# Probabilities times V for two query blocks in one product of 256 columns

## The chip, the core and the metric

One NeuronCore of a Trainium2 chip runs the whole program. The metric is the time of one execution on the device in microseconds (us). The profile covers one execution and gives the span from its first to its last instruction. Engines: PE is the matrix engine (TensorE), PEld its loads of weights, DVE the vector engine, ACT the scalar engine, POOL is GpSimd, and SP issues most of the DMAs.

## What is computed

Two layers over 512 latent tokens (a grid of 8 rows by 64 columns) and 256 context tokens, width 1024. In each layer the normed tokens go through one projection into three groups of heads side by side: neighbourhood attention (4 heads of 64, called NA below), a state-space mixer in both directions (SSD) and attention with shared keys and values (4 query heads, 2 key heads, called GQA). One output projection joins them, then a SwiGLU block follows. The part that the change touches is the last line of each attention:

```python
def gqa_softmax_attention(q, k, v):
    s = jnp.einsum('bqgrd,bkgd->bgrqk', q, k) * (HEAD_DIM ** -0.5)
    p = jax.nn.softmax(s.astype(jnp.float32), axis=-1).astype(v.dtype)
    return jnp.einsum('bgrqk,bkgd->bqgrd', p, v)
```

Neighbourhood attention is the same over a window of keys with a bias and the context keys. Context tokens see context keys only. In the second layer the context tokens have no output.

## The kernel before

A scheduler puts each engine's instructions into one fixed order when the program is built; priorities follow the order in which the code is written, and a tile's buffers (a tag and a count) limit how far work runs ahead. On the chip each engine takes its own list in order and waits at semaphores.

Each layer has three stretches: projections, the attention stage, and the output projection with the feed-forward block. The attention stage of layer 0 takes 301 to 470 us of the span, that of layer 1 takes 1290 to 1423 us. In it the units of attention, the SSD core, the gate and the loads of the next stage are interleaved by a table (`UCFG`) that says at which unit each event is written.

`attn` handles two heads (`j`) and two blocks of 128 queries (`qi`), four units. Each layer calls it for two pairs of NA heads and two pairs of GQA heads, and for each pair for two halves of the tokens and, in layer 0, for the context: 20 calls in all, 12 in layer 0 and 8 in layer 1. A unit's `scores` (lines 390, 393) write to PSUM tile `S`; DVE takes the maximum; ACT writes exponentials to `pr` (line 410); POOL scales them (line 415). `transposes` turns `pr` by identity matmuls on PE into PSUM tile `PT` (line 424), and ACT or DVE copies that to SBUF (lines 428, 430): tiles `PHA` for head 0 and `PHB` for head 1, one for each block of queries. `values` (line 436) multiplies by V. It has V as the stationary operand, 64 columns of the array for each head (`tile_position`), so that head 0 uses the left half of the array and head 1 the right half, and 128 columns of transposed probabilities stream through for each of 5 (NA), 6 (GQA) or 2 (context) key tiles. Every product is float32 and appears in the trace as two passes. `yout` copies the result out of PSUM tile `sm`: for NA by ACT (lines 622, 625) with one DMA for both blocks, for GQA by `split` into a rounded part on ACT (line 282) and the rest on DVE (line 283).

The loop at lines 1095 to 1104 writes for unit i: scores of unit i+2, events, normalising of unit i+1, transposes of unit i, events, and then the pending product of the unit before:

```python
            units[i][2][2]()
            events(i + 0.5)
            if pend:
                pend()
            pend = units[i][2][3]
```

Other work that is spoken of: `diag` (SSD within a chunk) loads two tiles `wh`, `wl` from `crow` (line 884), forms decays on DVE (line 892) and multiplies on PE (lines 913, 914), whose end frees the two tiles for the next load; line 958 forms states and line 971 what tokens see of them, both full-array products of 256 columns. `mod_chunk` (line 178) multiplies modulation weights with 32 columns of the array for each of four products. `PHA` and `PHB` also hold four of the eight low parts of the normed tokens (`h_tiles`), and early on weights of the modulation.

Of the kernel before, what the change touches and what calls it, by code (L numbers as in the profile page):

```python
# [8 lines left out]
F32 = mybir.dt.float32  # L9
F32R = mybir.dt.float32r  # L10
# [4 lines left out]
P = 128  # L15
D = 1024
KB = 8
# [11 lines left out]
def hybrid_kernel(ctx: ExitStack, tc: tile.TileContext, a, out, dbg=None):  # L29
# [18 lines left out]
    HT = ["HY"] * 4 + ["HS"] * 4 + ["HZ"] * 4 + ["PHA"] * 2 + ["PHB"] * 2  # L48
    GT = ["GV"] * 2 + ["GX"] * 4 + ["GB"] * 2 + ["GT"] * 2 + ["GC"] * 2 + ["GK", "GR", "GR", "GR"]
    BUFS = {t: (XT + HT + GT).count(t) for t in XT + HT + GT}  # L50
    BUFS.update(XFB=2, YO=1, HD=1)
# [33 lines left out]
    class Split:  # L85
        """columns 0 .. 511 in one bank of PSUM, the others in another"""
# [20 lines left out]
    # ---------------------------------------------------------- constants  # L107
# [42 lines left out]
    # ---------------------------------------------------------- modulation  # L150
# [8 lines left out]
    def mod_loads(l, c, tags):  # L159
        """512 columns of the modulation weights in tiles of the given tags, one or two k per tile"""  # L160
        w, k = [], 0
        for tag in tags:
            if tag in WB:
                wt, n = T(sb, tag, WB[tag], [P, 2, 512]), 2
            else:
                wt, n = T(sb, tag, BUFS[tag], [P, 1, 512]), 1
# [6 lines left out]
    def mod_chunk(l, c, w):  # L173
        """columns 512 c .. 512 c + 511 of the modulation; four row groups of the array take four k"""
# [21 lines left out]
    def mod_rows():  # L196
        """silu of both conditioning vectors as rows on every partition, in four tiles (vector, half)"""
# [11 lines left out]
    def mod_dots(l, c, rows, ptile, aside):  # L209
        """the same columns as mod_chunk by products along rows of the transposed weights"""  # L210
# [50 lines left out]
    # ---------------------------------------------------------- helpers  # L261
# [26 lines left out]
    def h_tiles():  # L288
        return [slot(HT[d], F32R) for d in range(KB)], [slot(HT[8 + d], F32R) for d in range(KB)]

    def spread(rstd, n):
        """per-token values as a row on every partition"""
# [10 lines left out]
    def make_h(l, xT, h, pbs, part, shi, sc):  # L303
        """norm, scale and shift of one part of the tokens"""
# [25 lines left out]
    def proj_ws(pt, wh, wl, xh, xl, nk, segs, ks=None):  # L330
        """pt[:, seg] = W^T x, W stationary (nk blocks of 128 rows)"""
# [13 lines left out]
    def proj_as(pt, ws, n, kper, xh, xl, t):  # L345
        """pt[:, :n] = x[t]^T W, activations stationary"""
# [28 lines left out]
    def attn(V2, xk, kts, qcols, bias, yout):  # L375
        """two heads and two blocks of queries; xk: range of x keys (or None); kts: key tiles for P V.
        Returns the steps of the four units: scores and softmax, transposes, and P V where one is complete"""
# [39 lines left out]
        def transposes(j, qi):  # L417
            t_ = ph[j, qi] = slot("PH" + "AB"[j], F32, (P, 6, P))
# [13 lines left out]
        def values(qi):  # L432
# [60 lines left out]
    for l in range(L):  # L493
# [109 lines left out]
        def na_sets():  # L603
            for b in range(2):
# [7 lines left out]
                for half in range(nhalf):  # L612
                    yt = []

                    def yout(pv, qi, b=b, half=half, yt=yt):
                        if qi == 0:
                            yt.append(sb_())
# [753 lines left out]
```

## Time and profile before

| | us |
|---|---|
| median of 3 runs | 1846.74 (1846.3 to 1852.83) |
| span of the profiled execution | 1843.3 |
| PE busy in the span | 1737.0 (94%) |
| attention stage of layer 0: length, PE busy | 168.6, 149.98 |
| attention stage of layer 1: length, PE busy | 132.5, 119.05 |

The page gives no time of the profiled execution besides its span; the span lies 3.4 us below the median of the runs. PE has a record for each pass, its busy time counts overlapping passes once, and a pass in flight counts as busy, so a busy PE can still be slowed by gaps between starts. The chain is the work that ended last, followed back step by step; a piece in it runs from its own start or release to that of the next piece.

### The profile page before, as it was taken

The page shows a single profiled execution, that of the slowest core. Times are in us where ns is not written, and L with a number is a line of the kernel's source. Part 1 is how long each engine was busy: PE and PEld are TensorE (multiplying, and loading weights), DVE is VectorE, ACT ScalarE, POOL GpSimd, SP SyncE. Part 2 cuts the span into 40 slices and gives each one's busy share as a digit, 9 for nine tenths or more (in the row PEclk, how much of TensorE's full clock was granted, in tenths as well). Part 3 has the DMA queues.
Part 4 walks back from the last instruction along what each step waited for, and adds up shares of the span by engine and source line. Part 5 has one row for each costly group of instructions (what it writes and reads, how often), then busy time and mean ns, then how long its engine had stood idle before and what let it go on. Part 6 is the DMA issues. An engine that isn't in the chain of part 4 may idle for free.

```text
span 1843.3 us, 26677 instructions
## 1 busy us (share of the span) xinstructions
PE 1737.0 (94%) x10146; PEld 1478.4 (80%) x10146; DVE 1104.0 (60%) x2209; ACT 681.5 (37%) x1386; POOL 423.1 (23%) x429
## 2 busy tenths in 40 slices
PE   7987778989999999999999999999899999999998
PEld 3887667777878888888888887989677788888887
DVE  4559996877475555455654576587786743333334
ACT  5554555556344221121112224334555442232222
POOL 0488886654010000000000002241653100000000
PEclk9998889989989999999999999999999999999999
DMA  9542526433123334333443454342631323333332
GB/s 368 201 139 103 163 89 186 140 90 106 56 75 115 114 115 126 103 116 107 124 129 102 130 163 139 96 131 79 183 105 53 108 90 93 99 96 92 103 100 83
DMA packets 94319, 221.66 MB, mean 120 GB/s; under 512 B 18416, under 2 KB 26224, under 8 KB 94192
## 3 DMA queue, kind: packets, MB, share of 16 engines
q1 hardware_dynamic: 78096, 204.65, 35.6%
q10 hardware_dynamic: 16096, 15.31, 2.5%
q8 instruction: 80, 1.31, 0.3%
q14 instruction: 47, 0.39, 0.1%
HBM read 198.49 MB, written 21.43 MB: 119 GB/s over the span
## 4 chain that ended last, share of the span: by engine, by line
PE 76%; DVE 11%; DMA 5%; ACT 3%; issue 2%; POOL 2%; SPq 0%; ACTq 0%; DVEq 0%; POOLq 0%
PE S L338 61%; PE sm L436 3%; DVE MB L768 2%; DMA wl<-crow 2%; PE PT L424 2%; DVE wl L327 1%; PE PT L338 1%; PE PT L352 1%; PE sm L352 1%; DMA wr<-in_mod_wT_dram 1%; DVE wh L892 1%; PE S L390 1%; ACT wh L326 1%; PE sm L913 1%; PE sm L914 1%
## 5 line engine op out<-in xcount | busy, mean ns | idle before, releaser
L326 ACT ACTIVATE wh<-wr 128x1024 fp32r<-128x1024 f32 (+3 forms) x214 | 207.6, 972 | 732.2 <-PE S L338 542.4
L327 DVE TENSOR_TENSOR wl<-wr,wh 128x1024 fp32r<-128x1024 f32 (+3 forms) x214 | 250.0, 1169 | 174.0 <-ACT wh L326 171.6
L269 POOL TENSOR_TENSOR tiny<-tiny,mhalf 128x2 f32<-128x2 f32 (+2 forms) x17 | 28.7, 1688 | 1067.5 <-DVE tiny L1160 1020.3
L338 PE MATMUL S<-HY,wh 128*128 128x512 f32 (+1 forms) x716 | 214.0, 357 | 5.9 <-ACT HY L318 4.1
L338 PE MATMUL S<-HY,wl 128*128 128x512 f32 (+1 forms) x716 | 214.5, 357 | 0.0
L338 PE MATMUL S<-HZ,wh 128*128 128x512 f32 (+1 forms) x716 | 212.8, 355 | 0.8 <-DVE HZ L319 0.8
L338 PE MATMUL S<-HS,wl 128*128 128x512 f32 (+1 forms) x716 | 213.1, 355 | 0.0
L338 PE MATMUL S<-HS,wh 128*128 128x512 f32 (+1 forms) x716 | 211.1, 353 | 0.0
L231 DVE CUSTOM_DVE_ANT_0 PT<-wr,XFB 128x512 f32<-128x512 f32 x112 | 75.5, 715 | 179.8 <-DMA wr<-in_mod_wT_dram 179.8
L338 PEld LDWEIGHTS S<-HY,wh 128*128 128x128 f32 x716 | 119.8, 192 | 27.2 <-ACT HY L318 4.4
L338 PEld LDWEIGHTS S<-HZ,wh 128*128 128x128 f32 x716 | 118.2, 191 | 21.7 <-DVE HZ L319 2.2
L338 PEld LDWEIGHTS S<-HS,wh 128*128 128x128 f32 x716 | 118.8, 191 | 20.2
L338 PEld LDWEIGHTS S<-HY,wl 128*128 128x128 f32 x716 | 118.8, 191 | 18.8
L338 PEld LDWEIGHTS S<-HS,wl 128*128 128x128 f32 x716 | 118.0, 190 | 18.6
L338 PE MATMUL S<-PHA,wh 128*128 128x512 f32 (+1 forms) x358 | 106.4, 355 | 0.0
L338 PE MATMUL S<-PHB,wh 128*128 128x512 f32 (+1 forms) x358 | 105.0, 351 | 0.0
L338 PE MATMUL S<-GX,wh 128*128 128x512 f32 (+1 forms) x400 | 97.2, 349 | 0.4 <-DVE KA L1114 0.4
L415 POOL TENSOR_SCALAR pr<-pr,tiny 128x640 f32<-128x640 f32 (+2 forms) x80 | 69.3, 869 | 84.0 <-DVE tiny L414 64.3
L768 DVE SCALAR_TENSOR_TENSOR MB<-MA,c,MB 128x770 f32<-128x770 f32 (+1 forms) x64 | 85.3, 1333 | 1.4
L228 POOL TENSOR_TENSOR KA<-QN,XFB 128x512 f32<-128x512 f32 x48 | 73.9, 1546 | 44.3 <-ACT XFB L205 23.5
L424 PE MATMUL PT<-c,pr 128*128 128x128 f32 x384 | 66.5, 289 | 13.4 <-POOL pr L415 4.6
L1261 DVE TENSOR_TENSOR MB<-S,MA 128x768 f32<-128x768 f32 (+1 forms) x42 | 34.6, 823 | 72.6 <-PE S L338 72.5
(402 smaller groups left out, 3911.7 us busy)
## 6 DMA issues: line engine op xcount, KB each, us to landing
wr<-in_mod_wT_dram SPq DMA_DIRECT2D x56, 512.0 KB, 3.7
wr<-in_w_gate_dram SPq DMA_DIRECT2D x44, 512.0 KB, 3.5
wr<-in_w_up_dram SPq DMA_DIRECT2D x44, 512.0 KB, 3.5
wr<-in_w_blk_dram SPq DMA_DIRECT2D x28, 512.0 KB, 3.6
wr<-in_w_down_dram SPq DMA_DIRECT2D x32, 448.0 KB, 3.3
QN<-in_mod_wT_dram SPq DMA_DIRECT2D x48, 256.0 KB, 3.3
wr<-in_w_out_dram SPq DMA_DIRECT2D x32, 256.0 KB, 2.6
wr<-in_w_down_dram SPq DMA_DIRECT2D x16, 512.0 KB, 3.4
```

The lines of the kernel that those rows point to most:

```text
L228: G.tensor_tensor(out=p_, in0=wv, in1=x, op=ALU.mult)
L231: V.tensor_tensor_reduce(out=p_, in0=wv, in1=x, scale=1.0, scalar=0.0, op0=ALU.mult, op1=ALU.add, accum_out=acc[:, o : o + 1],)
L269: POW.tensor_tensor(out=y, in0=v, in1=mhalf[:, 0:n], op=ALU.pow)
L326: S.activation(hi, raw, AF.Copy)
L327: V.tensor_tensor(lo, raw, hi.bitcast(F32), ALU.subtract)
L338: ins = PE.matmul(pt[:, c0:c1], lhsT=w, rhs=xx[:, c0:c1], start=(k == (0 if len(order) == 1 else order[0]) and i == 0), stop=(k == (nk - 1 ...
L352: PE.matmul(pt[:, 0:n], lhsT=s, rhs=w[:, o : o + n], start=(k == 0 and i == 0), stop=(k == KB - 1 and i == 2),)
L415: G.tensor_scalar(out=p_, in0=p_, scalar1=m[:, 4:5], scalar2=1.0, op0=ALU.mult, op1=ALU.mult)
L424: PE.transpose(pt[:, k * P : (k + 1) * P], pr[j, qi][:, kk * P : (kk + 1) * P], ident)
L436: PE.matmul(pv[64 * j : 64 * j + 64, 0:P], lhsT=V2(kts[k], j), rhs=ph[j, qi][:, k, :], start=(k == 0), stop=(k == nkt - 1), tile_position= ...
L768: V.scalar_tensor_tensor(ac[:, 0:wid], cp[:, j : j + wid], convw[l][:, b, j : j + 1], ac[:, 0:wid], ALU.mult, ALU.add)
L1261: V.tensor_tensor(gg[:, c0:c1], pu[:, c0:c1], sg[:, c0:c1], ALU.mult)
```

## The change

`values` runs once for each pair of heads, after the transposes of both query blocks, with 256 columns streaming instead of 128. The transposed probabilities of a head lie in one tile of two blocks (`PH`, three buffers of two blocks each, where `PHA` and `PHB` had two buffers of one block each). `yout` copies 256 columns at once. The low parts of normed tokens and the early modulation weights use halves of `PH`. A scratch area for DMA descriptors is made smaller; comments are gone, so line numbers behind line 170 differ by up to six.

```diff
-    HT = ["HY"] * 4 + ["HS"] * 4 + ["HZ"] * 4 + ["PHA"] * 2 + ["PHB"] * 2
+    HT = ["HY"] * 4 + ["HS"] * 4 + ["HZ"] * 4 + ["PH"] * 4
...
-    BUFS.update(XFB=2, YO=1, HD=1)
+    BUFS.update(XFB=2, YO=1, HD=1, PH=3)
...
-            if tag in WB:
-                wt, n = T(sb, tag, WB[tag], [P, 2, 512]), 2
+            if tag in WB or tag == "PH":
+                wt, n = T(sb, tag, WB.get(tag, 3), [P, 2, 512]), 2
...
-        return [slot(HT[d], F32R) for d in range(KB)], [slot(HT[8 + d], F32R) for d in range(KB)]
+        hi, lo = ([slot(HT[8 * i + d], F32R) for d in range(4 if i else KB)] for i in range(2))
+        for _ in range(2):
+            t = slot("PH", F32R, (P, 2, NT))
+            lo += [t[:, 0, :], t[:, 1, :]]
+        return hi, lo
...
-            t_ = ph[j, qi] = slot("PH" + "AB"[j], F32, (P, 6, P))
+            if qi == 0:
+                ph[j] = slot("PH", F32, (P, 2, 6, P))
+            t_ = ph[j][:, qi]
...
-        def values(qi):
+        def values():
             pv = ps_sm()
             for k in range(nkt):
                 for j in range(2):
                     PE.matmul(
-                        pv[64 * j : 64 * j + 64, 0:P], lhsT=V2(kts[k], j), rhs=ph[j, qi][:, k, :],
+                        pv[64 * j : 64 * j + 64, 0:256], lhsT=V2(kts[k], j), rhs=ph[j][:, :, k, :],
                         start=(k == 0), stop=(k == nkt - 1), tile_position=(0, 64 * j),
                     )
-            yout(pv, qi)
+            yout(pv)
...
-             lambda j=j, qi=qi: transposes(j, qi), (lambda qi=qi: values(qi)) if j else None, j)
+             lambda j=j, qi=qi: transposes(j, qi), values if j and qi else None, j)
...
-                            ov = yv.rearrange("p r c -> p c r")[:, 16 * qi : 16 * qi + 16, :]
-                            S.activation(ov, pv[:, 0:P].rearrange("p (c r) -> p c r", r=8), AF.Copy)
+                            S.activation(
+                                yv.rearrange("p r c -> p c r"), pv[:, 0:256].rearrange("p (c r) -> p c r", r=8), AF.Copy
+                            )
...
-                        split(yh[k][:, o : o + P], yl[k][:, o : o + P], pv[:, 0:P])
+                        split(yh[k][:, o : o + 256], yl[k][:, o : o + 256], pv[:, 0:256])
```

The scheduler gives a new order in both attention stages. PE's lists hold 384 products of line 436 before and 192 of line 442 now. These stand in 84 unbroken runs before and in 51 now.

First place: PE in layer 0, the first product of a pair of NA heads. Before, one of the two query blocks (result `sm_3111`) stands as one early product, not shown, and these two runs with transposes between them:

```order
L436 MATMUL sm_3111<-PHB_3060,GV_1042 64x128
L436 MATMUL sm_3111<-PHA_2998,GV_1042 64x128
L436 MATMUL sm_3111<-PHB_3060,GV_1042 64x128
L436 MATMUL sm_3111<-PHA_2998,GV_1042 64x128
L436 MATMUL sm_3111<-PHB_3060,GV_1042 64x128
L436 MATMUL sm_3111<-PHA_2998,GV_1042 64x128
L424 MATMUL PT_3093<-c_66,pr_3020 128x128 x2
L436 MATMUL sm_3111<-PHB_3060,GV_1042 64x128
L436 MATMUL sm_3111<-PHA_2998,GV_1042 64x128
L436 MATMUL sm_3111<-PHB_3060,GV_1042 64x128
L390 MATMUL S_3173<-KA_2861,QN_2858 128x384
```

Now both blocks together (result `sm_3139`), again behind one early product that is not shown:

```order
L442 MATMUL sm_3139<-PH_3053,GV_1036 64x256
L442 MATMUL sm_3139<-PH_2992,GV_1036 64x256
L442 MATMUL sm_3139<-PH_3053,GV_1036 64x256
L442 MATMUL sm_3139<-PH_2992,GV_1036 64x256
L442 MATMUL sm_3139<-PH_3053,GV_1036 64x256
L442 MATMUL sm_3139<-PH_2992,GV_1036 64x256
L430 MATMUL PT_3126<-c_66,pr_3044 128x128 x2
L442 MATMUL sm_3139<-PH_3053,GV_1036 64x256
L442 MATMUL sm_3139<-PH_2992,GV_1036 64x256
L442 MATMUL sm_3139<-PH_3053,GV_1036 64x256
L430 MATMUL PT_3166<-c_66,pr_3076 128x128 x3
```

The two runs cover one query block before and both blocks now; the second block's own two runs, which came next before, are gone.

Second place: PE in layer 0, the first product of `diag` (lines 913, 914 before, 915, 916 now; result tile `sm`, operands `MA`, `wh`, `wl`). Before:

```order
L424 MATMUL PT_3147<-c_66,pr_3051 128x128 x2
L436 MATMUL sm_3160<-PHB_3087,GV_1042 64x128
L436 MATMUL sm_3160<-PHA_3024,GV_1042 64x128
L436 MATMUL sm_3160<-PHB_3087,GV_1042 64x128
L393 MATMUL S_3215<-KA_2852,QN_2849 128x256
L393 MATMUL S_3215<-KB_2855,QN_2849 128x256
L913 MATMUL sm_3205<-MA_3108,wh_2992 128x64
L914 MATMUL sm_3205<-MA_3108,wl_2993 128x64
L913 MATMUL sm_3205<-MA_3108,wh_2992 128x64
```

Now:

```order
L960 MATMUL PT_3046<-XFB_3002,GB_2240 128x256
L960 MATMUL PT_3046<-XFB_3002,GB_2322 128x256
L442 MATMUL sm_3139<-PH_2992,GV_1036 64x256
L915 MATMUL sm_3184<-MA_3100,wh_2986 128x64
L916 MATMUL sm_3184<-MA_3100,wl_2987 128x64
L915 MATMUL sm_3184<-MA_3100,wh_2986 128x64
L916 MATMUL sm_3184<-MA_3100,wl_2987 128x64
L915 MATMUL sm_3184<-MA_3100,wh_2986 128x64
L916 MATMUL sm_3184<-MA_3100,wl_2987 128x64
```

Before, it stands behind all runs of the first pair's two query blocks (the last one is in the rows); now it stands behind one early product only, ahead of the pair's other nine.

Third place: SP in layer 0, loads of decays (`crow`, line 884 before, 886 now) among loads of keys and queries and of the bias table (`in_rpb_dram`). Before:

```order
L597 DMA GR_3548<-in_rpb_dram 128x384 x2
L884 DMA wh_3388<-crow_2527 128x512
L884 DMA wl_3389<-crow_2530 128x512
L358 DMA KA_3358<-nk_920 64x768 x2
L358 DMA KB_3361<-nk_922 64x768 x2
L358 DMA QN_3885<-gq_2076 64x768
L358 DMA QN_3885<-gq_2078 64x768
L358 DMA KA_3367<-nk_920 64x768 x2
L358 DMA KB_3370<-nk_922 64x768 x2
L358 DMA QN_3888<-gq_2076 64x768
L358 DMA QN_3888<-gq_2078 64x768
L884 DMA wh_3516<-crow_2527 128x512
```

Now:

```order
L886 DMA wh_3353<-crow_2521 128x512
L886 DMA wl_3354<-crow_2524 128x512
L603 DMA GR_3505<-in_rpb_dram 128x384 x2
L362 DMA KA_3323<-nk_914 64x768 x2
L362 DMA KB_3326<-nk_916 64x768 x2
L362 DMA QN_3814<-gq_2070 64x768
L362 DMA QN_3814<-gq_2072 64x768
L886 DMA wh_3474<-crow_2521 128x512
L886 DMA wl_3475<-crow_2524 128x512
L362 DMA KA_3332<-nk_914 64x768 x2
L362 DMA KB_3335<-nk_916 64x768 x2
L362 DMA QN_3817<-gq_2070 64x768
```

The two loads of a chunk stand one load of the bias table earlier in the first case, and between the keys of the two heads in the second.

## Rows read from the trace of the kernel before

**Rows 1.** The page: span, and the chain that ended last, by engine.

```profile
span 1843.3 us, 26677 instructions
...
PE 76%; DVE 11%; DMA 5%; ACT 3%; issue 2%; POOL 2%; SPq 0%; ACTq 0%; DVEq 0%; POOLq 0%
```

**Rows 2.** Windows of both attention stages: busy us of each engine, PEclk, DMA.

```profile
301.40:470.00 168.60, 149.98 (x1116) 120.42 (x1116) 128.58 (x359) 100.26 (x281) 94.65 (x123) 0.95 0.39 117
1290.50:1423.00 132.50, 119.05 (x896) 94.57 (x896) 99.27 (x262) 75.32 (x194) 70.00 (x88) 0.97 0.39 114
```

**Rows 3.** Line 436: one group of its matmuls, and one idle time ahead.

```profile
L436 PE MATMUL sm<-PHA,GV x176: 272/273/472, 303.9 to 1360.2; 128*64 128x128 f32 x176
...
  ACT PHB L428: 2.3, 2
```

**Rows 4.** The chain at 404 to 414 us: start, length, engine, line, instructions.

```profile
404.51 1.45 PE sm L436 x22
...
408.79 0.81 PE sm L436 x12
409.59 0.48 PE PT L424 x3
...
411.31 0.33 PE PT L424 x3
411.64 0.87 PE PT L971 x4
...
413.15 0.22 PE sm L913 x2
```

**Rows 5.** The chain in 301 to 470 us, its shares by line.

```profile
by line: PE sm L436 16.4%; PE PT L424 11.3%; DMA wl<-crow 7.3%; PE S L390 6.7%; PE S L393 5.3%; PE sm L913 5.1%; PE sm L914 5.0%; DVE wh L892 4.6%; PE S L338 4.1%; DMA zsp<-SA 3.7%; PE PT L971 3.5%; PE PT L958 3.3%; issue 2.8%; ACT pr L410 
```

**Rows 6.** The chain in 1290 to 1423 us, its shares by line.

```profile
by line: PE sm L436 15.9%; DMA wl<-crow 13.0%; PE PT L424 11.3%; DVE wh L892 7.1%; PE S L390 5.6%; PE S L338 5.1%; PE PT L958 3.9%; PE sm L913 3.9%; PE sm L914 3.8%; DVE tiny L407 3.4%; PE PT L971 3.4%; POOL HY L920 3.0%; issue 2.6%; PE S L
```

**Rows 7.** The chain in the first half of the first attention stage.

```profile
324.14 0.58 PE sm L436 x6
...
327.40 4.11 DMA wl<-crow
```

**Rows 8.** The chain in the first half of the second attention stage.

```profile
1306.21 2.32 PE sm L436 x18
...
1314.58 6.09 DMA wl<-crow
```

**Rows 9.** Windows of 20 us: busy us of each engine, PEclk, DMA.

```profile
380.00:400.00 20.00, 16.05 (x99) 12.57 (x98) 15.83 (x40) 11.66 (x31) 11.24 (x14) 0.94 0.34 100
400.00:420.00 20.00, 19.82 (x145) 15.39 (x144) 15.07 (x42) 10.36 (x29) 12.28 (x15) 0.89 0.23 74
```

**Rows 10.** The chain again: six passes of transposes at two clocks.

```profile
399.87 1.28 PE PT L424 x6
...
439.20 0.66 PE PT L424 x6
```

**Rows 11.** Groups of ACT in 301 to 470 us, by shape.

```profile
L428 ACT ACTIVATE PHA<-PT 128x256 f32<-128x256 f32 x12 | 4.6, 383 | 5.9 <-PE PT L424 5.9
...
L622 ACT ACTIVATE SB<-sm 128x128 f32<-128x128 f32 x8 | 3.2, 405 | 2.2 <-PE sm L436 2.2
...
L282 ACT ACTIVATE GV<-sm 128x128 fp32r<-128x128 f32 x6 | 1.7, 276 | 0.5 <-PE sm L436 0.5
```

**Rows 12.** A group of DVE in 301 to 470 us, by shape.

```profile
L283 DVE TENSOR_TENSOR GV<-sm,GV 128x128 fp32r<-128x128 f32 x6 | 1.7, 281 | 0.0
```

**Rows 13.** The timeline of PE: column-tiled matmuls of 512 columns.

```profile
31.74 1.06 PE L178 MATMUL S<-HS,cs 128*32 128x512 f32 x6
```

**Rows 14.** Waits of PE in the first attention stage: total us, times, longest.

```profile
PE sm L436 <- ACT PHB L428: 1.0, 1, 1.0
```

**Rows 15.** DMA issues of the page: KB each, us to landing.

```profile
wr<-in_mod_wT_dram SPq DMA_DIRECT2D x56, 512.0 KB, 3.7
...
QN<-in_mod_wT_dram SPq DMA_DIRECT2D x48, 256.0 KB, 3.3
```

More of the change, by code (lines that the diff above doesn't have):

```diff
@@ L483, in hybrid_kernel @@
         load_tok(tb)
-    mw = [mod_loads(0, 1, ["wh", "wl", "XFB", "XFB", "YO", "HD"]), mod_loads(0, 3, HT[4:8] + HT[12:16])]
+    mw = [mod_loads(0, 1, ["wh", "wl", "XFB", "XFB", "YO", "HD"]), mod_loads(0, 3, HT[4:8] + ["PH"] * 2)]
     ssq1 = tiny(6)
@@ L612, in na_sets, with yout @@
                 for half in range(nhalf):
[L613 to L617, printed above, removed]
-                        yv = yt[0]
+                    def yout(pv, b=b, half=half):
+                        yv = sb_()
                         if half < 2:
                             yv = yv.rearrange("p (r c) -> p r c", r=8)
-                            ov = yv.rearrange("p r c -> p c r")[:, 16 * qi : 16 * qi + 16, :]
-                            S.activation(ov, pv[:, 0:P].rearrange("p (c r) -> p c r", r=8), AF.Copy)
+                            S.activation(
+                                yv.rearrange("p r c -> p c r"), pv[:, 0:256].rearrange("p (c r) -> p c r", r=8), AF.Copy
+                            )
                             ydst = ydr[b][:, 0:512].rearrange("p (r c) -> p r c", c=64)[:, :, 32 * half : 32 * half + 32]
                         else:
-                            S.activation(yv[:, qi * P : qi * P + P], pv[:, 0:P], AF.Copy)
+                            S.activation(yv, pv[:, 0:256], AF.Copy)
                             ydst = ydr[b][:, 512:768]
-                        if qi == 1:
-                            nc.scalar.dma_start(ydst, yv)
+                        nc.scalar.dma_start(ydst, yv)
                     if half < 2:
@@ L731, in gqa_sets, with yout @@
                 for half in range(nhalf):
-                    def yout(pv, qi, g=g, half=half):
+                    def yout(pv, g=g, half=half):
                         k = 6 + g
@@ L735, in yout @@
                             yh[k], yl[k] = (mb([P, NT], F32R) if g else slot("GV", F32R) for _ in range(2))
-                        o = 256 * half + P * qi
-                        split(yh[k][:, o : o + P], yl[k][:, o : o + P], pv[:, 0:P])
+                        o = 256 * half
+                        split(yh[k][:, o : o + 256], yl[k][:, o : o + 256], pv[:, 0:256])
                     if half < 2:
@@ L1360 @@
     arrs = _layout(inputs)
-    nc = _bacc.Bacc("TRN2", target_bir_lowering=False, num_devices=1)
+    nc = _bacc.Bacc("TRN2", target_bir_lowering=False, num_devices=1, dynamic_dma_scratch_size=1024)
     arrays, aps = {}, {}
```

## Prediction

> **What bounds the kernel now.** I read the page first. The chain that ended last runs through PE for 76% of the span [rows 1], so time that leaves PE's list counts, if PE was what the stage waited for at that point. The windows of the two attention stages come next, since only there does line 436 run: PE is busy 149.98 of 168.60 us and 119.05 of 132.50 us, and 18.6 and 13.5 us are idle [rows 2]. Both stages are PE's, with holes. Then the chain inside them, by line: line 436 holds 16.4% of the first (27.7 us) and 15.9% of the second (21.1 us), the largest share of any line in both [rows 5, 6]. Together 48.8 us, which is all that the change can work on directly. The loads of decays stand on the same chain with 7.3% and 13.0% [rows 5, 6]: there PE waits, and a faster PE gains nothing.
>
> **What a product of 128 columns costs.** A recorded pass of line 436 takes 272 ns [rows 3], but passes overlap, so its price is the distance between starts, read from pieces of the chain. Products of the two heads that stand next to each other in the list use different halves of the array and start together; I call one such start a round. A piece of 22 records takes 1.45 us and one of 12 takes 0.81 [rows 4]. The longer one is a whole GQA product (6 key tiles, two heads, two passes: 24 passes, two of them without a record), 12 rounds, the shorter one is half of that, 6 rounds. So six rounds take 0.64 us and one 0.107. The shorter piece takes 0.81, which is 0.17 us more: that is paid when PE enters a run of line 436. Leaving costs as well: three transposes right behind the run take 0.48 us, three others 0.33 [rows 4], 0.15 more. A run costs 0.32 us beside its rounds.
>
> Counted in PE's order, before has 84 runs and 222 pairs or single products of two passes, 444 rounds; the change has 51 runs and 116, 232 rounds. Before, line 436 costs 444 x 0.107 + 84 x 0.32 = 47.5 + 26.9 = 74.4 us of PE. The chain holds 48.8 of them, 66%; I take the same share of whatever is saved.
>
> **What a product of 256 columns costs.** The trace has none with half of the array. The nearest row is line 971, full array, 256 columns, four passes in 0.87 us, 0.217 each [rows 4]: twice 0.107. A lower bound is that the pass stays at 0.107: line 913 streams 64 columns and costs 0.11 a pass (two in 0.22) [rows 4], hardly more or less than 128 columns, so below 128 columns there is a price that the columns don't set, and it might reach further up. An upper bound is that the two halves no longer run side by side, 0.43 for a round; against that, six products of 512 columns with 32 columns of the array each take 1.06 us [rows 13], 0.18 each, which is less than 0.217 for twice the columns, so tiles of the array do run side by side at longer streams. I take 0.217, since two rows of the full array (64 and 256 columns) put the floor below 256. Rounds: 232 x 0.217 = 50.3, against 47.5: +2.8 us. More than nothing, as some products of the two heads are apart in either order.
>
> The Trainium skill, "TensorE: Matmul & The Clock Gate", section "Back-to-back issue gap", speaks for more: it gives some 81 ns for a sustained matmul of 128 columns and 131 for 512. A line between them gives 98 for 256, 1.21 times as much and not twice; by it a round would cost an estimated 0.130 us, and the sum below would end near 1826.6 us. The trace disagrees between 128 and 256 columns on different tilings (0.107 against 0.217); it has no pair with the same tiling.
>
> **Runs.** 33 fewer, x 0.32 = -10.6 us. With the rounds -7.8 us of PE, and 66% of that on the path: **-5.1 us**.
>
> **End of a stage.** The last copy behind the last product covers 256 columns instead of 128. ACT takes 276 ns for 128 columns out of PSUM and 383 for 256 [rows 11], +0.11. DVE's half takes 281 for 128 [rows 12]; with ACT's ratio +0.11 (bounds: nothing, if it hides behind ACT, and twice, +0.28). Two stages: **+0.4 us**.
>
> **Earlier `diag` products, later loads.** In the new order the first products of `diag` stand ahead of most of the first pair's products. Their end frees `wh` and `wl`, and the next loads from `crow` can start; these are on the chain with 4.11 us at 327.40 and 6.09 at 1314.58 [rows 7, 8]. What stands on the chain ahead of the freeing and now behind it is products of line 436: 0.81, 0.58, 0.81, 0.58 in the first stage (2.8 us in four pieces, the last is shown) and 2.32, 0.81, 0.58 in the second (3.7, the first is shown) [rows 7, 8]. Bounds 0 and -6.5. SP's order puts loads of keys between these loads at other places, which works either way. I take a third, **-2.1 us**, for the products that are passed must still run and only those that would have filled the wait are gained.
>
> **What I cost at nothing.** The copies: 20 calls with one copy instead of two save 2 x 276 - 383 = 169 ns each on ACT [rows 11], 3.4 us in all, and about half of that on DVE; ACT is idle for two fifths of the stages and DVE for a quarter (100.26 and 128.58 us busy of 168.60 in the first) [rows 2], PE covers them, and if that cover went they would be a gain. NA's copies (405 ns [rows 11]) likewise. The modulation loads into `PH` are two of 512 KB instead of four of 256: 3.7 us to landing instead of 3.3 [rows 15]; +0.4 us once at most. Three buffers of `PH`: a call takes two, so the next call's tile for head 1 waits for this call's product, which the code writes ahead of the transposes that fill that tile, on the same engine; if it waited all the same, the price is one copy, 0.383 us [rows 11]. The smaller scratch area for descriptors: no row shows it. The new wait: a product of block 0 now waits for block 1's copies as well, with the next scores and transposes queued behind it on PE and DVE's maxima behind those. But the last product stands as far behind its own copies as before, one unit, and there such waits are rare: two in the whole program, 2.3 us, ACT's copy of `PHB` the last to come [rows 3], one of 1.0 us in the first stage [rows 14]. 0, with an upper bound of 20 x 1.0.
>
> **Sum.** -5.1 + 0.4 - 2.1 = -6.8 us. The profiled execution spans 1843.3 us, which gives 1836.5; the median lies 3.4 us above that span, so **1839.9 us**. I count 0.5% (9.2 us) as what a measurement of this kernel can tell from no change: 1837.5 and 1856.0 are the bounds.
>
> **Rivals.**
>
> *Swallowed.* One more load of decays gets onto the chain because of its new place in SP's order, or one of those there gets longer. Price: one such piece, 6.1 us [rows 8]. For it: these loads hold 7.3% and 13.0% of the chain [rows 5, 6], and PE's saving elsewhere only makes it reach them sooner. Against it: most pairs of them stand earlier, not later, relative to PE's work. 1839.9 + 6.1 = 1846.0 us, no change to be told.
>
> *All on the path, and a warm stretch.* The order of the saved work is regular, and 0.66 of it is an average: if every saved microsecond counts, -7.8 instead of -5.1. Besides, PE's granted clock is 0.94 in 380 to 400 us and 0.89 in 400 to 420 [rows 9]. With levels of 2.4 and 1.2 GHz that is 2.4 and 4.4 us at the lower level, and six transposes there take 1.28 us instead of 0.66 [rows 10]; half of 6.8 us, 3.4 us, would come back if the hole ahead of it (16.05 us busy of 20 [rows 9]) closes. -7.8 + 0.4 - 2.1 - 3.4 = -12.9: 1833.8 us.
>
> *Columns free up to 256.* A round stays at 0.107: 232 x 0.107 = 24.8, -22.7 on rounds, with the runs -33.3, x 0.66 = -22.0, and with the other terms -23.7: 1823.0 us. For it only the flat price from 64 to 128 columns [rows 4], against it line 971. The Trainium skill's rule above would end near this case.
>
> *Slower: products wait for the second block.* If each of the 20 products waits 1.0 us as the one in [rows 14] does, PE's list stands still for 20 us, the sum is +13.2 and the time 1859.9 us. It decides (slower by more than 9.2) from 0.80 us each: (9.2 + 6.8) / 20. For it: the first block's product used to fill PE's list while the second block's copies came, and that filling is gone. Against it: [rows 3] has two such waits among 40 products.
>
> **How the numbers follow.** The forecast, with its own range of 1836 to 1844 from the bounds of its terms near the middle, has 0.45; swallowed 0.22; all on the path 0.17; columns free 0.06; slower 0.10. The range leaves out the last two: 1831 to 1852, a few us around the outer of the other cases. Faster by more than 0.5%: all on the path, columns free and a sixth of the forecast (0.08), together 0.31. Slower 0.10. Same 0.59.
>
> **What the profile after would show.** Right: a round of the new line at 0.20 to 0.23 us in the chain, the line's share of both stages' chains lower by 2 to 3% of the stage; the first stage shorter by 3 to 5 us, the second by 2 to 3; the rest of the program within 1 us; PE's idle time ahead of the new product ended by copies of `PH` at 3 us or less in all; the load of decays near 327 and 1314 us shorter or gone. Wrong: passes at 0.13 us or at 0.43; waits for `PH` on PE over 10 us; a longer piece of `wl<-crow`; a longer stretch at a granted clock below 0.9; or a change outside the attention stages, for which I have no term.

## The result, and the profile after

The changed kernel takes **1857.63 us** (median of 9 runs, 1853.82 to 1862.96) against 1846.74 us, ratio **1.0064** (95% interval 1.005 to 1.0078): about 11 us slower, where 7 us faster was forecast. Runs with a disturbed clock are left out of all comparisons here.

The page of the changed kernel, the two lines that answer to [rows 1]:

```profile
span 1855.5 us, 25856 instructions
...
PE 75%; DVE 13%; DMA 6%; ACT 3%; issue 2%; POOL 1%; SPq 0%; ACTq 0%; DVEq 0%
```

The span is 12.2 us longer with 821 instructions fewer. To see where, I cut both programs at the same events: from the first product of `diag` in a layer (line 897 before, 899 now) to the first sum of squares behind its output projection. These stretches are longer than the windows of [rows 2] and hold the whole attention stage with the projection behind it. Windows of the kernel before (length, then busy us of PE, PEld, DVE, ACT, POOL, then PEclk, DMA share, GB/s):

```profile
302.60:532.10 229.50, 210.60 (x1461) 172.98 (x1460) 164.22 (x416) 119.25 (x311) 93.45 (x121) 0.96 0.34 104
1291.90:1462.00 170.10, 156.26 (x1077) 125.23 (x1076) 123.95 (x301) 90.66 (x220) 68.60 (x86) 0.98 0.38 111
```

and of the changed kernel:

```profile
303.80:539.10 235.30, 206.41 (x1254) 161.30 (x1253) 164.24 (x412) 118.77 (x299) 94.05 (x122) 0.96 0.34 101
1299.90:1474.00 174.10, 158.29 (x901) 122.75 (x900) 123.91 (x297) 89.58 (x212) 70.90 (x85) 0.93 0.37 107
```

The two stretches grow from 399.6 to 409.4 us, 9.8 of the 12.2; the other 2.4 lie elsewhere in the program, where the prediction had no term. PE's busy time falls by 2.2 us (366.9 to 364.7), and its idle time, length minus busy, rises from 32.7 to 44.7: **12 us of new holes**. In the second stretch the mean granted clock falls from 0.98 to 0.93. With the levels 1.2 and 2.4 GHz a mean of 0.93 over 174.1 us is about 24 us at the lower one, against 7 before. Over both stretches it is about 43 us against 25, and each of these 18 us can cost PE up to half of it. The two stretches lose in different ways. In the first the mean clock is 0.96 in both programs and PE's idle time grows by 10.0 us (18.9 to 28.9). In the second idle time grows by 2.0 us (13.8 to 15.8), and PE is busy for 2.0 us longer though it has less to do: there the loss is mostly the clock's.

The product itself is what was worked out. Pieces of the chain of the changed kernel, with the time of the stage's first half ahead of them:

```profile
320.91 4.37 DMA wl<-crow
...
334.19 6.54 DMA wl<-crow
...
382.21 5.93 DMA wl<-crow
...
415.35 1.45 PE sm L442 x12
416.80 0.48 PE PT L430 x3
...
420.67 0.33 PE PT L430 x3
...
464.18 2.73 PE sm L442 x22
```

12 rounds take 2.73 us and 6 take 1.45, so a round of 256 columns costs 0.213 us; a run costs 1.45 - 6 x 0.213 = 0.17 to enter and 0.48 - 0.33 = 0.15 to leave, as before. On the chain of the first stage the loads of decays have grown, which answer to [rows 7]. The shares of the chain in 302 to 474 us, which answer to [rows 5]:

```profile
by line: DMA wl<-crow 14.0%; PE sm L442 8.8%; PE PT L430 6.1%; PE sm L915 4.7%; DVE wh L894 4.6%; issue 4.4%; PE S L394 4.4%; PE sm L916 4.2%; PE S L342 3.5%; PE PT L973 3.3%; DMA zsp<-SA 3.1%; ACT wl L890 3.1%; PE PT L960 2.8%; PE S L397 2
```

P V (the product of probabilities and V, line 442) has 8.8% where it had 16.4%, the loads of decays 14.0% where they had 7.3%. More of the chain now runs through the loop of `diag` (load, ACT, DVE, PE, free tile, next load). That does not hold for the second stage, 1297 to 1434 us, which answers to [rows 6]. Nor does the loads' share follow the time: in the kernel with the change for GQA alone, which is no slower than the kernel before (below), they have 12.4% of the first stage's chain. The chain of the second stage, and that of GQA alone in 301 to 467 us:

```profile
by line: PE sm L442 17.4%; DMA wl<-crow 12.3%; PE PT L430 11.6%; PE S L394 9.5%; PE PT L960 6.7%; PE sm L915 5.7%; PE sm L916 5.6%; PE S L397 4.3%; PE S L342 4.1%; PE PT L973 3.5%; ACT pr L414 3.3%; ACT PH L434 1.8%; ACT wl L890 1.8%; issue
...
by line: DMA wl<-crow 12.4%; PE sm L452 9.5%; PE PT L430 9.4%; PE sm L442 5.6%; PE S L342 5.0%; PE sm L929 4.7%; PE sm L930 4.7%; POOL HY L936 4.4%; PE S L394 4.2%; DVE wh L908 3.5%; issue 3.5%; PE S L397 3.5%; PE PT L974 3.0%; DVE tiny L41
```

PE does not stand at the new product. Its waits in the first stage before, 301 to 470 us (total us, times, longest):

```profile
PE S L390 <- ACT pr L410: 7.1, 4, 6.2
PE PT L424 <- POOL pr L415: 3.3, 5, 1.8
PE PT L424 <- ACT PHB L428: 2.6, 2, 1.7
...
PE PT L971 <- ACT PHA L428: 0.4, 1, 0.4
```

and now, 302 to 474 us:

```profile
PE S L394 <- ACT pr L414: 9.0, 5, 5.7
PE PT L430 <- ACT PH L434: 3.5, 2, 2.7
PE PT L430 <- DVE HS L968: 3.3, 2, 2.3
PE PT L430 <- DVE PH L436: 2.7, 3, 1.4
PE PT L960 <- ACT PH L434: 2.5, 3, 1.5
PE PT L973 <- ACT PH L434: 2.0, 2, 1.1
PE sm L915 <- DVE tiny L412: 1.4, 1, 1.4
PE sm L899 <- DVE HY L918: 1.0, 1, 1.0
PE sm L915 <- DVE wh L910: 0.9, 1, 0.9
```

What the line of the product itself waited for in the whole program, before and then now (issue is time in which the engine waited for nothing that the profile shows):

```profile
  issue: 14.7, 63
...
  issue: 11.3, 48
  ACT PH L434: 0.7, 2
```

There are two waits for copies of `PH`, 0.7 us, where before had two of 2.3 [rows 3]. All the waits of PE in the first stage add up to 18.3 us before and 28.1 now. Most of them lie ahead of scores and transposes in both programs (16.2 and 20.3 us), but most of the growth lies ahead of the SSD core's products, lines 960, 973, 899 and 915: 7.8 us where there were 0.4. The engines waited for are ACT and DVE. Most of PE's idle time lies in the first half of the stage: windows of 100 us, before and then after.

```profile
300.00:400.00 100.00, 83.03 (x602) 67.44 (x601) 79.94 (x225) 57.93 (x165) 63.83 (x83) 0.94 0.48 141
400.00:500.00 100.00, 98.07 (x703) 80.35 (x702) 66.54 (x170) 51.57 (x136) 31.82 (x41) 0.98 0.24 77
```

```profile
300.00:400.00 100.00, 77.67 (x468) 58.02 (x467) 71.10 (x208) 50.88 (x141) 57.81 (x77) 0.91 0.49 137
400.00:500.00 100.00, 93.19 (x596) 72.47 (x596) 74.16 (x181) 57.53 (x146) 37.65 (x47) 1.00 0.24 77
```

From 300 to 400 us, where the NA heads and `diag` run together, all four engines do less: PE 5.4 us, DVE 8.8, ACT 7.1, POOL 6.0. No engine is full there, so the stretch is limited by waits. What DVE, ACT and POOL lack there they do from 400 to 500 us, and the stage ends later.

### The profile page after: what moved, and what is told of

It is laid out like the page before. It is cut to its first block, busy times and chain, and to the rows that moved or that the text cites. A ratio compares the mean times of both kernels' runs of the same rounds, so it can differ in the third digit from the quotient of the medians.

```text
span 1855.5 us, 25856 instructions
## 1 busy us (share of the span) xinstructions
PE 1736.3 (94%) x9762; PEld 1464.7 (79%) x9762; DVE 1101.6 (59%) x2199; ACT 680.1 (37%) x1366; POOL 424.9 (23%) x429
## 4 chain that ended last, share of the span: by engine, by line
PE 75%; DVE 13%; DMA 6%; ACT 3%; issue 2%; POOL 1%; SPq 0%; ACTq 0%; DVEq 0%
PE S L342 59%; DVE MB L770 3%; DMA wl<-crow 3%; PE sm L442 2%; PE PT L356 2%; DVE wl L331 2%; PE sm L356 1%; PE PT L430 1%; PE PT L342 1%; PE S L394 1%; DMA wr<-in_mod_wT_dram 1%; PE sm L915 1%; PE sm L916 1%; PE PT L960 1%; PE S L178 1%
## 5 line engine op out<-in xcount | busy, mean ns | idle before, releaser
L342 PE MATMUL S<-PH,wh 128*128 128x512 f32 (+1 forms) x716 | 211.1, 353 | 0.0
L342 PEld LDWEIGHTS S<-PH,wh 128*128 128x128 f32 x716 | 118.3, 190 | 20.1
L770 DVE SCALAR_TENSOR_TENSOR MB<-MA,c,MB 128x770 f32<-128x770 f32 (+1 forms) x64 | 82.6, 1290 | 1.4
```

What stands on the lines that cost most here:

```text
L342: ins = PE.matmul(pt[:, c0:c1], lhsT=w, rhs=xx[:, c0:c1], start=(k == (0 if len(order) == 1 else order[0]) and i == 0), stop=(k == (nk - 1 ...
L770: V.scalar_tensor_tensor(ac[:, 0:wid], cp[:, j : j + wid], convw[l][:, b, j : j + 1], ac[:, 0:wid], ALU.mult, ALU.add)
```

## The experiments

Ratios are to runs of the kernel before on the same chip, with 95% intervals. Theories on the way: **order** (P V is written later, so the scheduler puts `diag` ahead of it, and that costs), **buffers** (`PH`), **width** (256 columns as such), **readiness** (block 0's product is no longer there early), **loads** (the decays come late), **holes** (one coarse product for two blocks costs where PE has holes and gains where it is full).

**Tiles of the change, products of before.** `values` and `yout` as in the kernel before, `PH` as in the change.

> The tiles of the changed kernel (PH in three buffers of two blocks, the loads of 512 KB, the smaller scratch area), but P V in two products of 128 columns with two copies, written where they were before. The order of PE's list is that of before, row by row. Theory order (the time went because P V is written one unit later for block 0, which gives the scheduler another order with diag ahead of it): 1846 us, ratio 0.998 to 1.002. Theory buffers (tiles that hold both blocks come free later, or the larger early loads cost): most of the 11 us, 1853 to 1859 us, ratio 1.004 to 1.007.

1846.67 us, ratio 1.0009 (0.9996 to 1.0022). PE's list is that of before. The tiles, the 512 KB loads and the scratch area cost nothing that can be measured: buffers is out.

**Two products of 128 columns, one behind the other.**

```diff
-            for k in range(nkt):
-                for j in range(2):
...
-                        pv[64 * j : 64 * j + 64, 0:256], lhsT=V2(kts[k], j), rhs=ph[j][:, :, k, :],
...
+            for qi in range(2):
+                for k in range(nkt):
+                    for j in range(2):
...
+                            pv[64 * j : 64 * j + 64, P * qi : P * qi + P], lhsT=V2(kts[k], j), rhs=ph[j][:, qi, k, :],
```

> The changed kernel with the product at the same place in the code, but as two products of 128 columns one behind the other, in the two halves of the same PSUM tile, with one copy. Theory order: the place counts and not the width; 232 rounds of 0.217 become 444 of 0.107, so 1852 to 1862 us, ratio 1.003 to 1.008. Theory width (a pass of 256 columns costs more than two of 128, or the product of both blocks stands still until block 1 is copied): most comes back, 1844 to 1850 us.

1848.07 us, 1.0018 (1.0001 to 1.0035). Written at the same place with the same single copy, it gets most of the loss back: the later place in the code is not what costs.

**Block 0's product where it was, one copy.** The tiles and the single copy of the change, with `values(qi)` pending for each block, both into one PSUM tile.

> The tiles and the single copy of the changed kernel, but block 0's product (128 columns) written where it was before, one unit ahead of block 1's, into the first half of the same PSUM tile. Theory order: the cover that block 0's product gave comes back, 1843 to 1851 us, ratio 0.998 to 1.002. Theory merged copy (one of the two small PSUM tiles is held from the first product to the copy of both blocks, and diag, which uses the same two tiles, waits): as slow as the change or slower, 1855 to 1865 us, since the tile is held a unit longer still.

1849.76 us, 1.0036 (1.0019 to 1.0053). The time lies in the first theory's range, the ratio above it. Against the tiles alone (1.0009) that is some 5 us, not 11; the longer hold of the PSUM tile comes with another order, so the 5 us are not shown to be its price.

**P V ahead of the events.**

```diff
-            events(i + 0.5)
             if pend:
                 pend()
+            events(i + 0.5)
```

> The changed kernel, but the loop writes the pending P V ahead of the events of its half unit (steps of diag, state, gate) instead of behind them, so that P V stands ahead of diag in PE's list. Theory order, in the form that diag ahead of P V makes PE wait for decays that are not ready: half of the loss or more comes back, 1844 to 1852 us. Rival, any change of the order moves the time by a few us either way and this one is no better than another: 1850 to 1865 us.

1858.67 us, 1.0089 (1.0069 to 1.011). Nothing comes back, but the edit did not bring what its expectation says. In PE's list the first products of `diag` (lines 915, 916) still stand behind one early product and ahead of the pair's other nine, as in the changed kernel. The timeline of PE:

```profile
314.54 0.65 PE L442 MATMUL sm<-PH,GV 128*64 128x256 f32 x2
315.12 0.43 PE L915 MATMUL sm<-MA,wh 128*128 128x64 f32 x2
...
320.55 1.52 PE L442 MATMUL sm<-PH,GV 128*64 128x256 f32 x12
```

So this run does not test the order theory. The same edit in the kernel before as a control:

> The kernel before with nothing changed but that the loop writes the pending P V ahead of the events of its half unit. 210 of 8990 other instructions of PE stand elsewhere. It shows what a change of the order alone does to products of 128 columns. Theory order: several us to either side, 1840 or 1852 and beyond. Theory width: nothing much, 1843 to 1849 us.

1845.38 us, 1.0002 (0.9985 to 1.0019). This other order of products of 128 columns moves nothing that can be measured.

**Products of 128 columns, both blocks key tile by key tile.** The loops are `for k`, `for qi`, `for j`; start and stop once for each half of the array.

> The changed kernel with each product of 256 columns written as two of 128 right behind each other (key tile by key tile, block 0 and block 1), same tiles, same single copy. Of PE's other instructions 169 of 8990 stand elsewhere than in the changed kernel. Theory order (the list that the scheduler makes is what costs): as slow as the change, 1853 to 1860 us, ratio 1.004 to 1.008. Theory width (256 columns in one instruction, which needs both blocks at once, is what costs): 1845 to 1850 us, ratio 1.000 to 1.003, as the one with the blocks one behind the other (1848.1).

1856.69 us, 1.007 (1.0044 to 1.0096): as slow as the change, with no instruction wider than before. So width is out. What the slow ones share is that each key tile's step needs both blocks.

**Block 1 first.** As the two products one behind the other, with `for qi in (1, 0)`.

> Two products of 128 columns one behind the other, as in the run that took 1848.1 us, but block 1 first. Nothing else differs: same number and size of products, one copy, same place in the code. Block 0's product, ready a unit earlier, now stands behind block 1's and can't be used to fill PE's list. Theory readiness (what the change takes away is block 0's product as work that is ready early): as slow as the change, 1853 to 1860 us, ratio 1.004 to 1.008. Rival, the slow ones are slow by the accident of their order: 1845 to 1851 us.

1850.43 us, 1.0028 (1.0012 to 1.0045). Readiness wanted 1853 or more. Block 0 cannot be early here, and still more than half of the loss is gone. Readiness as I put it falls. The interval overlaps that of block 0 first (1.0001 to 1.0035), so the two cannot be told apart, and a part of it may stand.

This run tests order as well. Its first products of `diag` (lines 916, 917 here) also stand behind one early product of P V (line 443) and ahead of the pair's next run:

```profile
317.32 0.43 PE L443 MATMUL sm<-PH,GV 128*64 128x128 f32 x2
317.68 0.43 PE L916 MATMUL sm<-MA,wh 128*128 128x64 f32 x2
...
323.83 0.88 PE L443 MATMUL sm<-PH,GV 128*64 128x128 f32 x12
```

With block 0 first it is the same (`diag` at 311.38 us, between products at 305.78 and 321.73). `diag` ahead of P V is therefore not enough for the loss.

**The table.** `UCFG` with `diag` one unit later (1, 43 and 1, 29), with a second unit in layer 1 (1, 43 and 2, 30), and with all ends 5% earlier.

> The changed kernel with the table's steps of diag one unit later in both layers (the first two entries 1, 43 and 1, 29 for 0, 42 and 0, 28). Theory order, in the form that diag ahead of P V makes PE wait: diag's products move behind P V again, 1843 to 1852 us. Theory width: the order doesn't matter much, 1853 to 1862 us.

> The changed kernel with diag one unit later in layer 0 and two units later in layer 1 (one unit in both took 1852.2 us). Theory readiness: P V has moved by up to one unit, so diag moved by one fits in layer 0 and a second unit in layer 1 gives back part of what is left there, 1845 to 1851 us. Rival, the second unit makes diag the last of the stage: 1853 to 1862 us.

> The changed kernel with all events of the table but the starts about 5% earlier (40, 42, 44, 45, 46 for 42, 44, 46, 47, 48 in layer 0, the same by two units in layer 1). 455 of 8990 other instructions of PE stand elsewhere. Theory order: the time moves by several us, to either side, 1845 to 1865 us. Theory width: it stays, 1854 to 1861 us.

1852.23 us (1.0041, 1.0024 to 1.0059), 1851.9 us (1.0027, 1.0013 to 1.0042) and 1856.78 us (1.0071, 1.0044 to 1.0098). A later `diag` gives back some 4 to 7 us by the ratios, though the interval of the first run still overlaps that of the change (1.005 to 1.0078); the second unit adds nothing that can be told; earlier ends change nothing. None reaches the kernel before. With `diag` one unit later its first products still stand ahead of the pair's (315.38 us, ahead of a run at 321.75), so the gain does not come from putting them behind P V.

**Without the loads of decays.** In `diag` the two loads are gone, and ACT reads a tile of ones and DVE the identity in their place. These kernels leave out the part of the output within a chunk:

```diff
...
-                nc.sync.dma_start(t.rearrange("p h t -> p (h t)"), crow[i][:, o : o + 512].to_broadcast([P, 512]))
...
-                S.activation(Wb[:, h, :], Wb[:, h, :], AF.Identity, bias=ncum[:, c, o : o + 1])
+                S.activation(Wb[:, h, :], ones, AF.Identity, scale=-1.0e4, bias=ncum[:, c, o : o + 1])
...
-                V.scalar_tensor_tensor(E[:, h, :], E[:, h, :], ncum[:, c, o : o + 1], Wb[:, h, :], ALU.add, ALU.min)
+                V.scalar_tensor_tensor(E[:, h, :], ident, ncum[:, c, o : o + 1], Wb[:, h, :], ALU.add, ALU.min)
```

> The kernel before with the loads of decays left out of diag: ACT and DVE form them from a tile of ones instead (so the part of the output within a chunk is left out), all other work as it was. To be compared with the next one. The loads hold 7.3% and 13.0% of the two stages' chains, so some 10 us at most come back: 1836 to 1846 us.

> The changed kernel with the loads of decays left out of diag in the same way. Theory loads (PE is held up by diag's products, moved ahead, whose decays come late because of their loads, 27 us of the chain in the first stage against 12 before): without them the change gains what it was worth on PE, 4 to 8 us faster than the kernel before without loads. Theory readiness (PE lacks work to fill any wait, whichever it is): still 6 to 12 us slower than the kernel before without loads.

1839.84 us (0.9968, 0.9955 to 0.9981) and 1839.6 us (0.9963, 0.9945 to 0.9982): the loss is gone, and no gain appears. Windows of the two stretches, the kernel before without loads:

```profile
302.00:529.50 227.50, 211.99 (x1463) 173.65 (x1461) 163.39 (x413) 117.79 (x304) 91.68 (x118) 0.96 0.28 79
1289.80:1457.40 167.60, 156.07 (x1078) 125.86 (x1077) 123.96 (x300) 89.28 (x216) 68.70 (x85) 0.97 0.32 89
```

and the changed kernel without loads:

```profile
304.10:529.10 225.00, 205.15 (x1253) 160.08 (x1252) 163.38 (x408) 117.17 (x293) 94.38 (x120) 0.98 0.28 80
1292.20:1459.60 167.40, 154.05 (x903) 118.54 (x901) 122.32 (x296) 88.70 (x208) 68.95 (x85) 0.97 0.32 89
```

PE is busy for 359.2 us instead of 368.1, 8.9 less, and idle for 33.2 instead of 27.0, 6.2 more. The clocks are closer here, but not equal: by the means about 28 us at the lower level before and 19 with the change, so up to half of these 9 us of the saving can be the clock's. The new holes take most or all of what is left. The second profile is of a run 3.3 us above its median, so the balance is rough.

**One group of heads only.** Both blocks at once for the GQA heads, then for the NA heads; the other group in two products of 128 with two copies.

> Tiles of the changed kernel; products of both blocks (256 columns, one copy) for the GQA heads only, NA's as before in two of 128. Theory holes (the change costs where PE has holes, which is mostly the first half of each stage, NA with diag and its loads, and gains where PE is full, GQA): 1841 to 1847 us, ratio 0.997 to 1.001. Rival, coupling two blocks costs in both halves alike: 1849 to 1854 us.

> The other half: products of both blocks for the NA heads only, GQA's as before. Theory holes: all of the loss, 1855 to 1861 us, ratio 1.005 to 1.008. Rival, alike in both halves: 1849 to 1854 us.

1843.76 us (0.9983, 0.9966 to 1.0001) and **1862.38 us** (1.0087, 1.0072 to 1.0103). In GQA the change is not told from no change (2.5 us faster, with 1 inside the interval), in NA it is a loss of 16 us. Windows of the two stretches, GQA alone:

```profile
302.80:527.50 224.70, 205.04 (x1350) 165.28 (x1349) 164.78 (x410) 118.17 (x304) 95.41 (x121) 0.98 0.36 107
1286.40:1454.30 167.90, 152.76 (x982) 119.69 (x981) 125.72 (x297) 89.68 (x216) 71.75 (x85) 0.99 0.38 112
```

and NA alone:

```profile
303.20:541.90 238.70, 213.25 (x1366) 169.61 (x1365) 164.65 (x417) 119.42 (x305) 91.01 (x122) 0.95 0.34 100
1301.60:1478.10 176.50, 160.83 (x997) 127.02 (x996) 123.91 (x302) 89.93 (x216) 69.24 (x87) 0.93 0.37 106
```

With GQA alone PE is busy for 357.8 us and idle for 34.8, with NA alone 374.1 and 41.1. NA alone has less to do than the kernel before (366.9) and is busy for longer. Its clock is lower: about 49 us at the lower level in the two stretches against 25 before, and half of these 24 us is more than the 7.2 by which PE is busy longer. The profile of GQA alone (about 12 us at the lower level) is of a run 4.6 us below its median.

**NA alone without the loads.**

> 256 columns for the NA heads only, as in the run of 1862.4 us, with the loads of decays left out of diag as in the two runs of 1840.1 and 1839.6 us (the part of the output within a chunk is left out). Theory holes behind the loads (NA's coarser products cost because ACT and PE stand at the loads and nothing small is there to fill): the loss of 16 us nearly goes, 1838 to 1846 us. Rival (NA's product costs by itself, since it waits for both blocks): 1850 us and more.

1838.8 us (0.9968, 0.9956 to 0.9981), the ratio of the kernel before without loads. All of NA's loss needs the loads. Its windows:

```profile
301.80:526.90 225.10, 206.61 (x1365) 166.04 (x1364) 161.43 (x414) 117.07 (x298) 93.39 (x119) 0.98 0.28 80
1287.60:1450.90 163.30, 152.85 (x999) 119.09 (x997) 121.91 (x300) 89.13 (x212) 69.91 (x85) 1.00 0.32 91
```

PE is busy for 359.5 us in place of 374.1, at clocks of 0.98 and 1.00 in place of 0.95 and 0.93, and 12 of the 41 us of idle time are gone. This profile is of a run 3.5 us below its median.

**A fourth buffer for `wh` and `wl`**, in the kernel before (with the smaller scratch area) and in the changed one:

> The kernel before with four buffers of wh and wl instead of three (with the smaller scratch area, which makes room), so that a load of decays waits for the products of four steps of diag ago and not three. The tiles also hold projection weights. Theory loads: part of what the loads cost there comes back, 1838 to 1846 us. Rival: no change, 1843 to 1849 us.

> The changed kernel with four buffers of wh and wl instead of three. Theory loads (their buffers come free too late in the new order): most of the loss goes, at most 4 us slower than the kernel before with four buffers. Theory holes (PE lacks small pieces of work whatever it waits for): still 7 to 12 us slower than that.

1837.54 us (0.995, 0.9931 to 0.9968) and 1852.05 us (1.0032, 1.002 to 1.0045), 14.5 us apart. The buffer helps both by 5 to 9 us and the change costs as much as ever: the number of buffers is not what the loads' part in it rests on. The tiles hold projection weights too, so the gain need not lie in `diag`; the profile of the first is of a run 11 us above its median (1848.93 us) and can't tell.

**What was faster, together**: four buffers, both blocks at once for GQA alone.

> Both blocks at once for the GQA heads only (1843.8 us) with four buffers of wh and wl (1837.5 us with products as before). If the two gains are independent, 1833 to 1838 us, ratio 0.990 to 0.995; if the order that comes out spoils one of them, 1838 to 1846 us.

1843.59 us (0.9989, 0.9973 to 1.0005). The gains don't add: next to the four buffers alone the same edit in GQA is 6 to 7 us slower. The best kernel of the study stays the one before with a fourth buffer, 9 us faster than before and 20 faster than the change.

## Why the prediction was wrong

- **The price of a product was right.** 0.213 us for a round where 0.217 was taken; 0.32 us for a run, as taken. The Trainium skill, "TensorE: Matmul & The Clock Gate", section "Back-to-back issue gap", had led to an estimate of 0.130; with the same tiling the chip shows 0.107 and 0.213, twice for twice the columns. The costs of entering and leaving a run fit the Trainium skill, "TensorEngine Tiling (Array Packing)", section "Tiling Modes", by which a change of the tiling mode drains the engine; that is 0.17 and 0.15 us here, and no run shows that a drain is what they pay for.
- **The saving of PE fits, roughly.** -7.8 us was worked out; the pair without loads has -8.9, of which up to 4.6 can be the clock's.
- **The step that failed is what was costed at nothing: the new wait, that is, the tie between the two blocks.** The forecast took 66% of the saving as time, as if the chain's share of the line were a rate of exchange, and counted the loss of block 0's separate product as 0. In its place the runs show 12 us more idle time of PE and about 18 us more at the lower clock. The tie itself is measured by two runs of the same products of 128 columns: 1.0018 one block behind the other, 1.007 key tile by key tile. The share of P V on the chain was an average over a half in which PE has holes (83.03 us busy of 100) and a half in which it is full (98.07). NA's heads run in the first and lose 16 us, GQA's in the second and lose nothing that can be measured.
- **The slower rival had the time (1859.9 against 1857.6) and not the place.** It reckoned with 20 products that wait 1.0 us each. There are 0.7 us of such waits in all, so that the times agree is luck. The sign named for it, waits for `PH` on PE over 10 us, did come: 10.7 us in the first stage alone, where copies of `PHA` and `PHB` had 6.2. But they lie ahead of transposes and of lines 960 and 973, not ahead of the product, where the forecast looked for them. What has to be watched is the idle time of PE as a whole.
- **Earlier `diag`, -2.1 us, is not seen, and its sign stays open.** The loads on the chain went from 7.3% of 169 us (12 us) to 14.0% of 172 us (24 us, not the 27 that an expectation above names) in the first stage and from 13.0% to 12.3% in the second. The two kernels with one block behind the other have `diag` as early and are 3 to 5 us slower than the kernel before by their ratios, not faster. Putting `diag` a unit later helped, by 4 to 7 us.
- **The larger loads and the buffers at 0** hold: the tiles and loads alone measure 1.0009, although the loads into `PH` take 7.0 us to landing where those into `PHA` and `PHB` took 5.6 and 6.0, more than the +0.4 that rows of other tiles gave. The single copy and the end of a stage (+0.4) were not measured by themselves.
- **Other rivals.** *Columns free* is out: a round costs 0.213 us. *Swallowed* was right that a load of decays on the chain would get longer (6.54 us where the longest had 6.09), but not about the size of the loss. *A warm stretch* was right about the place, 380 to 420 us, which is now granted 1.00 where [rows 9] have 0.94 and 0.89, but not about the sum, for the first stretch as a whole has 0.96 as before. The window:

```profile
380.00:420.00 40.00, 32.01 (x204) 23.25 (x204) 27.18 (x71) 22.88 (x63) 20.65 (x29) 1.00 0.36 100
```

**What is shown and what is not.** Shown: the loss is NA's, it needs the loads of decays, more than half of it needs a product in which each key tile takes both blocks at once (in one instruction or in two), and it consists of idle time of PE and of its clock, which in the changed kernel's profile means idle time in the first stage and mostly the clock in the second. Argued only: why. That the holes are what sets NA apart from GQA is argued too, since the two also differ in bias, key tiles and copies. My reading is that in the half with `diag` the engines wait for one another in a circle through the loads, and the products of one block at a time are the small pieces that PE could do meanwhile. Against a simple form of it stands the run with block 1 first, in which nothing is ready early and which still took only 1850.4 us. Leaving the loads out also gives the scheduler another list, so it shows that the loss goes with the loads, not which wait carries it. ACT's waits for these loads do not settle it: in the whole program they are 28.8 us before, 37.4 with the change and 33.3 for NA alone, but 26.8 in the run of key tile by key tile, which is as slow as the change. Which wait it is stays open.

## What to carry to other kernels

The share of a line on the chain is not what a saving in it is worth. Cut the stage into the part where the engine is full and the part where it has holes, and be slow to count a saving in the second: without the loads PE's saving of 4 to 9 us came with 6.2 us of new holes. Ask what independent work the edit couples, and count idle time and granted clock over the whole stretch, since here the new waits showed at other instructions. An edit that applies to two kinds of calls is worth trying for each alone: here one changed nothing that can be measured and the other lost 16 us. And an edit in the code need not move what it names: one here left `diag` where it stood in PE's list.

## What was not expected of the hardware

The granted clock carries much of the loss in the second stage. The first 12 us of that stretch in the changed kernel, and the 12 behind them:

```profile
1300.00:1312.00 12.00, 8.32 (x34) 6.24 (x33) 8.87 (x27) 7.02 (x19) 7.90 (x10) 0.67 0.59 204
1312.00:1324.00 12.00, 11.76 (x66) 9.78 (x65) 7.42 (x25) 6.59 (x17) 6.37 (x9) 0.77 0.66 172
```

and in the kernel before, whose stretch starts 8 us earlier:

```profile
1292.00:1304.00 12.00, 7.61 (x37) 5.45 (x36) 8.88 (x28) 7.30 (x20) 8.19 (x11) 0.86 0.85 252
1304.00:1316.00 12.00, 11.13 (x86) 9.36 (x85) 6.64 (x25) 6.13 (x15) 7.08 (x10) 0.86 0.57 156
```

Both programs have PE busy for some 8 us of the first 12 and for over 11 of the next. The changed kernel is granted 0.67 and 0.77, the kernel before 0.86 and 0.86; with the two levels that is about 13 us at the lower one against 7. In the second window PE gets 66 instructions done in 11.8 busy us, before 86 in 11.1 (some of the 66 are twice as wide, and the lists differ). Busy time alone would have called this a full engine, and it does not tell the two clocks apart. In NA alone the lower clock outweighs the work that was saved: PE has less to do and is busy for 7 us longer.
